# Making twelve features' gate/up weight sums in the mixer, and Strassen down products in the first FFN block

## The chip, the cores and the metric

The kernel runs on one core of one Trainium2 chip. The metric is the device time of one launch in microseconds (us); smaller is better. A time shown for a kernel is the median of several runs.

## The reference, cut to what matters

```python
def hybrid_layer(x, ...):
    h = rmsnorm(x, norm1_w)
    proj = h @ w_in                      # q/k/v, z, a, b, pooling input
    ...                                  # gated delta rule (4 heads) and causal mean pooling (4 groups)
    x = x + concat([o_delta, o_pool]) @ w_out
    h = rmsnorm(x, norm2_w)
    x = x + (silu(h @ w_gate) * (h @ w_up)) @ w_down
    return x, ...
```

There is one layer, 2048 new tokens of a prompt and 64 tokens of a running stream (2112 in all), model width 1024 and FFN width 2816, all in float32. The kernel cuts the FFN width into 22 "features" of 128 columns.

## The kernel before, in words

**Precision.** Every large product is made of three TensorE products: an operand is split into a high part (a copy rounded to float32r, on ScalarE) and a low part (operand less high part, on VectorE); high times high, high times low and low times high are summed in PSUM. "Splitting" a tile is this pair of instructions, one on each engine.

**The mixer** is the first part of the program. It takes the tokens in four blocks of 512 (the first also holds the 64 stream tokens). The loop at lines 1375 to 1436 makes a block's projections head by head, runs the delta-rule chains of the heads beside them, and a block's output projection (`out_proj`, line 1291) is made during the next block. The weights of the projections are split once, kept in DRAM (`wnd`, `wod`) and loaded as 512 KB tiles `wsp` afterwards.

**The FFN** takes the tokens in three blocks of 704, numbered 0, 1 and 2. For each feature `gate_up` (line 1514) computes gate and up with a 2x2 Strassen scheme of seven products. It needs seven weight tiles: three are blocks of the weights as they are (`11`, `12`, `22`), four are sums (`S1` to `S4`). `prep_strassen` (line 582) makes them. In block 0 it loads four raw quarters of 256 KB (`wr`, `wrS`), makes the four sums on GpSimd, splits all seven tiles and stores the four split sums to DRAM (`gsd`, 512 KB each, "gS" in the trace). In blocks 1 and 2 the key is in `stored`, so it loads the four split sums (`wsS<-gS`), and only three raw quarters are loaded and split.

**Down.** The features form six groups of 4, 4, 4, 4, 2 and 4 (`FGROUPS`). A group's down product is made soon after its last gate/up. It has two forms, chosen by `plain` (line 504):

- the plain form (`down`, line 1561): eight weight tiles of 256 KB are loaded and split; each output tile takes, for each half of the tokens, three products per feature, so a group of four takes 8 x 2 x 4 x 3 = 192 matmuls, and VectorE adds 16 results to `y`. `gate_up` splits each feature's result itself.
- the Strassen form (`down_strassen`, line 1595, with `prep_down`, line 616, and `factors`, line 1572): pairs of features are combined, GpSimd makes four sums for a pair of features and four half-width sums for each of four weight tile pairs, more tiles are split, and a group of four takes 4 x 7 x 2 x 3 = 168 matmuls and 28 adds to `y`.

Before the change `SDOWN = (1, 2)`: block 0 uses the plain form everywhere, blocks 1 and 2 the Strassen form (block 2's last group is plain).

**What sets the order.** Nothing goes to the chip as it is written. `Machine` (line 59) records every instruction with the tiles that it reads and writes, and `issue` (line 183) makes one list schedule of the whole program: for each engine it picks, at each planned time, the ready instruction of lowest rank. Rank is the place in the program less `machine.boost`. Planned durations are in `cost` (line 140); a transfer counts as ready for its user 3 us after its planned landing (`MARGIN`); SyncE's transfers whose rank is far ahead of the front are held back until the planned wire is idle (`BACKLOG, IDLE, AHEAD_OPS`). A `Chain` (line 379) is a generator stepped by a rough TensorE clock, which sets where in the program its instructions stand. All transfers are issued by SyncE, in one order; each engine then runs its list in order.

Tiles come from pools with a fixed number of buffers per tag: `wraw` (four raw weight tiles), `wsp` (four split tiles, for projections and FFN alike), `op` (two, large), and the FFN's own pool `f2`, which opens when the mixer's pools `cp1` and `gp` are done.

Of the kernel before, what the change touches and what calls it, by code (L numbers as in the profile page):

```python
# [11 lines left out]
F32 = mybir.dt.float32  # L12
F32R = mybir.dt.float32r
AF = mybir.ActivationFunctionType
ALU = mybir.AluOpType
# [3 lines left out]
P = 128  # L19
# [21 lines left out]
TB2 = NTOK // NB2  # L41
# [3 lines left out]
SUBS2 = ((0, N2), (N2, N2))  # L45
FGROUPS = (4, 4, 4, 4, 2, 4)

SDOWN = (1, 2)

FW = ("11", "S1", "S2", "12", "S3", "S4", "22")  # L50
FH = ("11", "T1", "T2", "21", "T3", "22", "T4")
# [304 lines left out]
def hybrid_kernel(ctx, tc, a, o):  # L356
    nc = machine = Machine(tc.nc)
    act = nc.scalar.activation
    tt = nc.vector.tensor_tensor
# [72 lines left out]
    cpool, wpool, opool = pool("cpool"), pool("wpool"), pool("opool")  # L432
# [5 lines left out]
    cp1, gp = pool("cp1", p1, True), pool("gp", p1, True)  # L438
# [6 lines left out]
    gsd = {nm: dpool.tile([NF, P, 1024], F32, tag=f"g{nm}", name=f"g{nm}") for nm in KEEP}  # L445
# [49 lines left out]
    groups, f0 = [], 0  # L495
# [4 lines left out]
    def halves(b, gi):  # L500

        return ((0,), (1,)) if (b, gi) == (NB2 - 1, len(groups) - 1) else ((0, 1),)

    def plain(b, gi):
        return b not in SDOWN or len(halves(b, gi)) > 1

    order = []
    for b in range(NB2):
# [9 lines left out]
    ready, due, stored = [], [], set()  # L518
# [217 lines left out]
    def norm_stats(B):  # L736

        if B.j == 1:
            B.r = wpool.tile([P, 512], F32, tag="xc", name="rn1", bufs=XBUFS["xc"])
        else:  # L740
            B.r = cpool.tile([P, TB2], F32, tag="r", name=f"rn{B.j}")
        if B.j == 0:
            for _ in rstd("n1_0", B.r, from_x0, S0, gp, "ext", 4, nc.gpsimd, lambda name: bank(0, name)):
                pass
        else:
            Chain(rstd(f"n1_{B.j}", B.r, stream_x(a["xT"], "xa", B.t0), [(0, B.NB)], gp, "ext", 4, nc.gpsimd))
# [69 lines left out]
    names = {}  # L816
# [474 lines left out]
    def out_proj(B):  # L1291
        acts = [(k, B.o[k]) for k in (4, 5, 6, 7, 0, 1, 2, 3)]

        late = [0] if B.kept else []
        src = stream_x(a["xT"], "xc", B.t0, "xc")
        for ms in ((0, 1), *((m,) for m in range(2, KT))) if B.kept else ((m,) for m in range(KT)):
            ws = [weights("wout", m, *late) for m in ms]
            for lo, n in B.subs:
                xs = [src(m, lo, n) for m in ms]
                pss = [psmm(f"pz{B.j}_{m}_{lo}") for m in ms]  # L1300
                for part in (acts[:4], acts[4:]) if len(ms) > 1 else (acts,):
                    for w, ps in zip(ws, pss):
# [23 lines left out]
    def stats2(b, pool, tag, tbufs):  # L1326
# [18 lines left out]
        for k in range(4):  # L1345
# [20 lines left out]
            put("T4", k, t4)  # L1366
            yield LAT_APPLY

    heads = []
    blocks = []  # L1370
    prev = None
    for j in range(NBLK):
        first = None
        if j:
            pab, first = project(B, 0, 1)
        else:
            pab = project(B, 0)
        machine.boost = HOT_ROWS
        rows(B, pab)
        machine.boost = 0  # L1380
        blocks.append(B)
        nxt = Block(j + 1) if j + 1 < NBLK else None
        B.heads, B.pools = [], []
        if prev is None or nxt is None:
            new_o(B)
        for h in range(NH):
            B.heads += head_project(B, h, first if h == 0 else None)
            heads.append(B.heads[h])
            if h == 1 and nxt is None:
                pools(B)  # L1390
            if h == OUT_AFTER and prev is not None and nxt is not None:
                drain(lambda: all(g.done for g in prev.heads) and all(c.done for c in prev.pools))
                out_proj(prev)
                if not B.kept:
                    new_o(B)
            if h == 1 and j == 0:
                fold = Chain(fold_pool())
            if h == 1 and nxt is not None:
                norm_stats(nxt)
            if h == STATS0 and nxt is None:  # L1400
                stats0 = Chain(stats2(0, gp, "ext", 4))
        if j == 0:
            fold.wait()
        if nxt is not None:
            pools(B)
            norm_apply(nxt)
        prev, B = B, (nxt if nxt is not None else B)
# [23 lines left out]
    for k in (4, 5, 6, 7, 0, 1, 2, 3):  # L1431
        t = wpool.tile([P, 512], F32, tag="xc", name=f"od{k}", bufs=XBUFS["xc"])
        nc.sync.dma_start(out=t, in_=od[k])
        split(last_prev.o[k], slice(0, last_prev.NB), t)
    machine.boost = 0
    out_proj(last_prev)
    stats0.wait()
    hA = [bp.tile([P, 6, 2, N2], F32R, tag=f"h{i}", name=f"hA{i}") for i in range(2)]
# [75 lines left out]
    def gate_up(b, f):  # L1514
        w = weights("gu", f)
        tag = f"{b}_{f}"
        raw = f2.tile([P, 2, N2], F32, tag="hr", name=f"hr{tag}", bufs=3)

        def add(ps, nw, nh, first=False):

            for i, t in enumerate(hq[nh]):
                ks = slice(i * P, (i + 1) * P)
                for q, (wi, ai) in enumerate(((0, 0), (0, 1), (1, 0))):
                    mm(ps, w[nw][:, wi, ks], t[:, ai, :], start=first and i == q == 0, stop=i == 3 and q == 2,
                       skip_group_check=not first)
                pump()

        def sigmoid(e, x):
            act(e, x, AF.Exp, scale=-1.0)
            act(e, e, AF.Ln, bias=onec)  # L1530
            act(e, e, AF.Exp, scale=-1.0)

        def finish(i, g, u):
            e = raw[:, i]
            tt(e, e, g, ALU.mult)
            tt(e, e, u, ALU.mult)
            if b not in SDOWN:
                split(h3t[f % 6], slice(i * N2, (i + 1) * N2), e)


        x, y, z = (psg(f"p{i}_{tag}")[:, :N2] for i in "xyz")
        add(x, "11", "11", True)
        hurry(nc.scalar.copy, g1 := tmp(f"g1_{tag}"), x)
        add(y, "S1", "T1", True)
        hurry(nc.scalar.copy, u2 := tmp(f"u2_{tag}"), y)
        add(x, "S2", "T2")
        hurry(nc.scalar.copy, g2 := tmp(f"g2_{tag}"), x)
        add(z, "12", "21", True)
        hurry(tt, g1, z, g1, ALU.add)
        sigmoid(raw[:, 0], g1)  # L1550
        add(x, "S3", "T3")
        hurry(tt, u2, x, u2, ALU.add)
        add(y, "S4", "22")
        hurry(tt, g2, y, g2, ALU.add)
        sigmoid(raw[:, 1], g2)
        finish(1, g2, u2)
        add(x, "22", "T4")
        finish(0, g1, x)
        return raw if b in SDOWN else h3t[f % 6]

    def down(b, gi, h3, ys, which, done):
        f0, G = groups[gi]
# [48 lines left out]


    fpos = {2: (0, 1), 4: (0, 2, 1, 3)}
    six = [opool.tile([P, 3, 2, TB2], F32R, tag="op", name=f"h3_{i}", bufs=2) for i in range(2)]
    h3t = [six[i // 3][:, i % 3] for i in range(6)]
    h3, ys = {}, {}

    def between(b):
# [7 lines left out]
    for op in order:  # L1626
        b = op[1]
        if op[0] == "gu":
            f = op[2]
            if f == 0:  # L1630
                fill.finish()
            if op == ("gu", 0, 2):
                nxt = Chain(between(-1))
            h3[f] = gate_up(b, f)
            if b in SDOWN:
                gi = max(g for g, (f0, G) in enumerate(groups) if f0 <= f)
                if plain(b, gi):
                    if f == groups[gi][0] or f == groups[gi][0] + 2:
                        two = opool.tile([P, 2, 2, TB2], F32R, tag="op", name=f"h3l{f}", bufs=2)
                    for i in range(2):  # L1640
                        split(two[:, f % 2], slice(i * N2, (i + 1) * N2), h3[f][:, i])
                    h3[f] = two[:, f % 2]
                elif f % 2:
                    h3[f] = factors(b, f, h3.pop(f - 1), h3[f])
            if f == NF - 1 and b + 1 < NB2:
                nxt.finish()
                fill = Chain(load_h(b + 1, FH))
        else:
            f0, G = groups[op[2]]
            while b not in ys:  # L1650
                nxt.step()
            hs = [h3.pop(f0 + i) for i in range(G) if f0 + i in h3]
            if not plain(b, op[2]):
                down_strassen(b, op[2], hs, ys[b])
            for which in halves(b, op[2]) if plain(b, op[2]) else ():
                done = []
                if which != (0, 1):
                    Chain(last_norm(b, ys[b], *which, done))
                down(b, op[2], hs, ys[b], which, done)
            if op[2] == len(groups) - 1 and b + 1 < NB2:  # L1660
                nxt = Chain(between(b))
# [33 lines left out]
KEEP = ("S1", "S2", "S3", "S4")  # L1695
HOT_ROWS = BOOST
HPOOL = (0, 1, 2, 3)
LAT_LOAD = 0.6
WAIT_STAT = 8.46

# [111 lines left out]
```

## Time and profile before

| | |
|---|---|
| median of 3 runs | 2340.63 us (2338.54 to 2341.11) |
| the profiled execution's own time | 2338.61 us |
| its span in the trace | 2336.8 us |
| TensorE busy | 2301.8 us, 99% of the span |
| VectorE, ScalarE, GpSimd busy | 72%, 58%, 36% |
| moved by DMA | 471.36 MB, 202 GB/s over the span |

PE stands for TensorE's matmuls and PEld for its weight loads, DVE for VectorE, ACT for ScalarE, POOL for GpSimd, SP or SPq for SyncE's queue. Rows of a group of instructions read: line, engine, operation, output tile <- input tiles, shapes, count | busy us, mean ns of one | idle time of the engine before them and what ended it. Nearly all instructions have line 278, where the scheduler issues them, so one goes by tile names. Rows of a stretch of time read: its limits, its length, then for each engine the busy us with the number of instructions, the granted TensorE clock, the DMA engines' busy share and GB/s.

### The profile page before, as it was taken

To read this page: it belongs to the slowest core of one execution; us is meant where nothing else is said; L and a number is where in the kernel's file an instruction comes from. 1 tells how busy PE (TensorE), PEld (TensorE's weight loads), DVE (VectorE), ACT (ScalarE), POOL (GpSimd) and SP (SyncE) were. 2 spreads that over 40 slices of the span, in tenths; PEclk is the share of its full clock that TensorE was granted. 3 is DMA by queue.
4 is the path that set the end of the run, shared out by engine and by line. 5 is a ranking of instruction groups with operands and counts; after the bars stand their busy time and mean duration, and the time that the engine had idled before them with its cause. 6 is when DMAs were issued, how large, how long until landed. Compare 5 with 4: busy or idle time off the path is not lost.

```text
span 2336.8 us, 41455 instructions
## 1 busy us (share of the span) xinstructions
PE 2301.8 (99%) x14614; PEld 2138.4 (92%) x14614; DVE 1689.0 (72%) x3097; ACT 1356.4 (58%) x3020; POOL 843.6 (36%) x963
## 2 busy tenths in 40 slices
PE   8999999999999999999999999999999999999998
PEld 7898898778777878999999999999999999999998
DVE  8998755664676786788667665877877868766776
ACT  6987856683767675655445465554444664454444
POOL 3434222430234530554322244643432653331312
PEclk9999999999999999999999999999999999999999
DMA  8755566545464577877545377768545586455453
GB/s 293 250 160 181 169 229 209 182 156 192 165 212 159 185 206 239 294 274 252 205 169 187 139 247 231 240 205 285 181 142 183 175 289 220 146 182 189 145 193 105
DMA packets 218881, 471.36 MB, mean 202 GB/s; under 512 B 27184, under 2 KB 85552, under 8 KB 218672
## 3 DMA queue, kind: packets, MB, share of 16 engines
q1 hardware_dynamic: 218672, 468.71, 60.9%
q8 instruction: 115, 1.88, 0.3%
q14 instruction: 94, 0.77, 0.1%
HBM read 354.81 MB, written 113.80 MB: 201 GB/s over the span
## 4 chain that ended last, share of the span: by engine, by line
PE 82%; DVE 9%; ACT 4%; DMA 3%; issue 2%; POOL 0%; SPq 0%; POOLq 0%; DVEq 0%; ACTq 0%
PE px L278 19%; PE pp L278 16%; PE pz L278 12%; PE py L278 8%; PE d L278 8%; PE dx L278 6%; PE dy L278 3%; PE pk_p L278 2%; PE pt_p L278 2%; DVE hq L278 2%; PE dz L278 1%; DVE y L278 1%; PE gr_p L278 1%; PE py_p L278 1%; ACT hr L278 1%
## 5 line engine op out<-in xcount | busy, mean ns | idle before, releaser
L278 PE MATMUL pp<-h,wsp 128*128 128x512 f32 (+1 forms) x2480 | 561.0, 366 | 11.6 <-DVE wsp L278 10.3
L278 PEld LDWEIGHTS pp<-h,wsp 128*128 128x128 f32 x2480 | 400.5, 189 | 59.1 <-ACT wsp L278 8.9
L278 ACT CAST ws<-wr 128x512 fp32r<-128x512 f32 x198 | 122.0, 618 | 172.9 <-PE dx L278 49.6
L278 DVE TENSOR_TENSOR ws<-wr,ws 128x512 fp32r<-128x512 f32 x198 | 164.2, 831 | 57.3 <-ACT ws L278 51.8
L278 PE MATMUL d<-h,wsd 128*128 128x352 f32 x1056 | 170.5, 322 | 0.0
L278 PE MATMUL pz<-op,wsp 128*128 128x288 f32 (+1 forms) x768 | 169.9, 357 | 0.3 <-DVE op L278 0.2
L278 PEld LDWEIGHTS d<-h,wsd 128*128 128x128 f32 x1056 | 168.7, 188 | 0.4 <-DVE h L278 0.4
L278 ACT ACTIVATE hr<-g 128x352 f32<-128x352 f32 x132 | 65.7, 497 | 163.8 <-DVE g L278 163.5
L278 ACT CAST TV_p<-pt_p 128x512 f16<-128x512 f32 x192 | 111.1, 589 | 62.2 <-PE pt_p L278 61.7
L278 PE MATMUL px<-hA,ws 128*128 128x352 f32 x792 | 144.7, 322 | 0.7 <-DVE ws L278 0.7
L278 PE MATMUL py<-hB,wsS 128*128 128x352 f32 x792 | 143.8, 322 | 0.0
L278 PE MATMUL px<-hBT,wsS 128*128 128x352 f32 x792 | 139.6, 324 | 3.0 <-ACT g L278 2.6
L278 PE MATMUL pz<-hB,ws 128*128 128x352 f32 x792 | 142.5, 322 | 0.0
L278 PE MATMUL py<-hA,wsS 128*128 128x352 f32 x792 | 139.8, 322 | 0.0
L278 PE MATMUL px<-hBT,ws 128*128 128x352 f32 x792 | 138.1, 322 | 1.3 <-DVE u L278 1.3
L278 POOL TENSOR_TENSOR wrS<-wr,wrS 128x512 f32<-128x512 f32 x44 | 63.0, 1431 | 207.7 <-DMA wr<-in_wg_dram 64.2
L278 PE MATMUL px<-hA,wsS 128*128 128x352 f32 x792 | 137.8, 322 | 0.0
L278 PEld LDWEIGHTS px<-hBT,wsS 128*128 128x128 f32 x792 | 128.2, 188 | 7.4 <-ACT g L278 7.3
L278 PEld LDWEIGHTS px<-hA,ws 128*128 128x128 f32 x792 | 129.8, 188 | 1.2 <-DVE ws L278 1.0
L278 PEld LDWEIGHTS px<-hBT,ws 128*128 128x128 f32 x792 | 128.6, 188 | 2.3 <-DVE u L278 2.2
L278 PEld LDWEIGHTS py<-hB,wsS 128*128 128x128 f32 x792 | 129.8, 188 | 0.0
L278 PEld LDWEIGHTS pz<-hB,ws 128*128 128x128 f32 x792 | 129.6, 188 | 0.0
(686 smaller groups left out, 5606.3 us busy)
## 6 DMA issues: line engine op xcount, KB each, us to landing
wsS<-gS SPq DMA_DIRECT2D x176, 512.0 KB, 4.6
wsp<-wnd SPq DMA_DIRECT2D x126, 512.0 KB, 3.4
gS<-wsS SPq DMA_DIRECT2D x88, 512.0 KB, 4.4
wr<-in_wg_dram SPq DMA_DIRECT2D x132, 256.0 KB, 3.1
wnd<-wsp SPq DMA_DIRECT2D x42, 512.0 KB, 5.0
xd<-x2d SPq DMA_DIRECT2D x96, 176.0 KB, 3.8
wr<-in_wu_dram SPq DMA_DIRECT2D x66, 256.0 KB, 3.6
wrd<-in_wd_dram SPq DMA_DIRECT2D x56, 256.0 KB, 3.6
```

The costliest lines, as they stand in the source:

```text
L278: getattr(getattr(self.nc, op.eng), name)(*args, **kw)
```

## The change

A new generator `sums_ahead` makes and splits, for features 0 to 11 (`NPRE = 12`), the four sums during the mixer and stores them in `gsd`. It starts in the second token block, after the third head's projections were recorded, and is finished before the last `out_proj`. All its engine instructions and stores have `boost = -1500` (a later rank); each of its steps waits 4 us of the rough clock. It uses the four `wraw` buffers, a new single buffer `sa`, and the space of the constant `poolw`.

For these features block 0 then finds the key in `stored` and loads the split sums, as blocks 1 and 2 do. In block 0 the first three groups (features 0 to 11) use the Strassen down form; the last three stay plain. The tiles `h3t` of the plain form are allocated when first needed (feature 12) rather than ahead of the FFN.

```diff
-SDOWN = (1, 2)
+SPLIT0 = 3
...
     def plain(b, gi):
-        return b not in SDOWN or len(halves(b, gi)) > 1
+        return (b == 0 and gi >= SPLIT0) or len(halves(b, gi)) > 1
...
+    def sums_ahead():
+        gt = nc.gpsimd.tensor_tensor
+        for f in range(NPRE):
+            raw = {}
+            for src, nm, i in (("11", "wg", 0), ("21", "wu", 0), ("22", "wu", 1), ("12", "wg", 1)):
+                raw[src] = wpool.tile([P, 512], F32, tag="wraw", name=f"sa{src}_{f}", bufs=4)
+                nc.sync.dma_start(out=raw[src], in_=a[nm][f][:, i * 512 : i * 512 + 512])
+            yield LAT_SUMS
+            s1, s2, s3, s4 = raw["22"], raw["11"], raw["21"], raw["12"]
+            for i, (nm, out, x, y, op) in enumerate((
+                    ("S1", s1, raw["21"], raw["22"], ALU.add), ("S3", s3, raw["11"], raw["21"], ALU.subtract),
+                    ("S2", s2, s1, raw["11"], ALU.subtract), ("S4", s4, raw["12"], s2, ALU.subtract))):
+                machine.boost = -IDLE_RANK
+                gt(out=out, in0=x, in1=y, op=op)
+                machine.boost = 0
+                if nm != "S1":
+                    yield LAT_SUMS
+            for i, (nm, t) in enumerate((("S1", s1), ("S3", s3), ("S2", s2), ("S4", s4))):
+                machine.boost = -IDLE_RANK
+                if i % 2:
+                    hi = names["poolw"].bitcast(F32R)
+                else:
+                    hi = gp.tile([P, 512], F32R, tag="sa", name=f"sa{nm}_{f}", bufs=1)
+                nc.scalar.copy(hi, t)
+                tt(t.bitcast(F32R), t, hi.bitcast(F32), ALU.subtract)
+                for q, x in enumerate((hi.bitcast(F32), t)):
+                    nc.sync.dma_start(out=gsd[nm][f][:, 512 * q : 512 * q + 512], in_=x)
+                machine.boost = 0
+                yield LAT_SUMS
+            stored.add(("gu", f))
...
+            if (j, h) == (1, 2):
+                ahead = Chain(sums_ahead())
...
     machine.boost = 0
+    ahead.finish()
     out_proj(last_prev)
...
     def gate_up(b, f):
...
+        six = b == 0 and f >= groups[SPLIT0][0]
+        if six and not h3t:
+            h3t.extend(t[:, i] for t in (opool.tile([P, 3, 2, TB2], F32R, tag="op", name=f"h3_{i}", bufs=2) for i in range(2)) for i in range(3))
...
-            if b not in SDOWN:
+            if six:
                 split(h3t[f % 6], slice(i * N2, (i + 1) * N2), e)
...
-            if b in SDOWN:
-                gi = max(g for g, (f0, G) in enumerate(groups) if f0 <= f)
+            gi = max(g for g, (f0, G) in enumerate(groups) if f0 <= f)
+            if b or gi < SPLIT0:
                 if plain(b, gi):
...
+NPRE, IDLE_RANK, LAT_SUMS = 12, 1500, 4.0
```

More of the change, by code (lines that the diff above doesn't have):

```diff
@@ L1558, in gate_up @@
         finish(0, g1, x)
-        return raw if b in SDOWN else h3t[f % 6]
+        return h3t[f % 6] if six else raw
     def down(b, gi, h3, ys, which, done):
@@ L1613, in hybrid_kernel @@
     fpos = {2: (0, 1), 4: (0, 2, 1, 3)}
-    six = [opool.tile([P, 3, 2, TB2], F32R, tag="op", name=f"h3_{i}", bufs=2) for i in range(2)]
-    h3t = [six[i // 3][:, i % 3] for i in range(6)]
+    h3t = []
     h3, ys = {}, {}
```

## The prediction

> **What bounds the kernel now.** I read the page's head first, then busy time by stage, then the rate of TensorE's matmuls in each FFN block, then the waits.
>
> ```profile
> span 2336.8 us, 41455 instructions
> PE 2301.8 (99%) x14614; PEld 2138.4 (92%) x14614; DVE 1689.0 (72%) x3097; ACT 1356.4 (58%) x3020; POOL 843.6 (36%) x963
> ...
> PE 82%; DVE 9%; ACT 4%; DMA 3%; issue 2%; POOL 0%; SPq 0%; POOLq 0%; DVEq 0%; ACTq 0%
> ```
>
> TensorE is busy for 99% of the span and makes up 82% of the chain that ended last. The timeline of PE gives the borders of the FFN blocks: the first `px` matmul of blocks 0, 1 and 2.
>
> ```profile
> 946.10 2.08 PE L278 MATMUL px<-hA,ws 128*128 128x352 f32 x12
> ...
> 1414.34 2.08 PE L278 MATMUL px<-hA,ws 128*128 128x352 f32 x12
> ...
> 1867.83 1.61 PE L278 MATMUL px<-hA,ws 128*128 128x352 f32 x9
> ```
>
> The table by stretches then has the mixer's middle and the blocks 0 and 1:
>
> ```profile
> 330.00:820.00 490.00, 488.52 (x2977) 391.79 (x2975) 300.47 (x607) 312.03 (x749) 165.06 (x238) 1.00 0.57 186
> 946.10:1414.30 468.20, 466.95 (x2909) 465.28 (x2908) 332.87 (x511) 242.77 (x490) 182.52 (x142) 1.00 0.64 222
> 1414.30:1867.80 453.50, 448.57 (x2770) 443.03 (x2769) 348.91 (x595) 236.73 (x497) 193.89 (x199) 1.00 0.63 203
> ```
>
> In block 0 PE idles 1.25 of 468.2 us, and a matmul takes 468.2 / 2909 = 0.1610 us from start to start. In block 1, which already has what the change brings to block 0 (stored sums, Strassen down), it is 453.5 / 2770 = 0.1637 us. So time in the FFN is the number of matmuls, plus a little waiting that the Strassen form brings. In the mixer's middle PE idles 1.5 of 490 us. The clock is 1.00 in all three, so no term comes from it.
>
> **Part 1: fewer matmuls in block 0.** A group of four takes 168 instead of 192 matmuls; three groups remove 72. These are the ones removed:
>
> ```profile
> L278 PE MATMUL d<-h,wsd 128*128 128x352 f32 x1056 | 170.5, 322 | 0.0
> ```
>
> 170.5 / 1056 is 0.1615 us each, in agreement with block 0's rate, and no idle time stands before them. 72 x 0.1610 = **-11.6 us**. PE is the path here, so all of it counts.
>
> **Part 2: what the Strassen form gives back.** The three groups bring pair sums and weight sums on POOL, more splits on ACT and DVE, and 36 more adds to `y` on DVE, while 48 sums and their splits leave block 0. I need not add these up, since block 1 shows the finished mixture: DVE 348.9, ACT 236.7 and POOL 193.9 us of 453.5, no engine over 77%. What counts is the waiting that it causes. At block 1's rate the remaining 2909 - 72 = 2837 matmuls would take 2837 x 0.1637 = 464.5 us, and the gain would be only 3.7; at block 0's rate 11.6. These are the two ends. Block 1's surplus is 2770 x 0.0027 = 7.6 us. The waits of PE in 1414 to 1868 say where it is from, as far as they are named, and the timeline where two of them stand:
>
> ```profile
> PE px L278 <- ACT g L278: 1.8, 6, 0.5
> PE dz L278 <- DVE hq L278: 1.1, 1, 1.1
> PE dz L278 <- DVE y L278: 1.1, 2, 0.5
> PE dy L278 <- DVE y L278: 0.7, 1, 0.7
> ```
>
> ```profile
> 1845.98 0.43 PE L278 MATMUL dz<-hq,wsd 128*128 128x352 f32 x1 [1.07 <-DVE hq L278]
> ...
> 1860.35 1.23 PE L278 MATMUL dz<-hq,wsd 128*128 128x352 f32 x6 [0.54 <-DVE y L278]
> ```
>
> The waits of `dz` and `dy`, 2.9 us together, belong by these rows to the end of the block, where features run out and down products stand back to back; block 0's end stays plain. What is left, 4.7 us, I share by features: 12 of 22 is 2.6, and I take **+2.5 us** (ends 0 and 7.9). It is ScalarE's copy of `px` (`g`) coming late behind the splits of the pair tiles.
>
> **Part 3: what the mixer pays.** `sums_ahead` adds 48 sums on POOL, 48 copies on ACT, 48 subtractions on DVE, 48 loads and 96 stores of 256 KB. The same work in block 0 has these rows; the transfers are compared with loads of the same size:
>
> ```profile
> L278 POOL TENSOR_TENSOR wrS<-wrS,wr 128x512 f32<-128x512 f32 x44 | 63.8, 1451 | 29.6 <-DMA wr<-in_wu_dram 12.7 <-DVE hr L278 6.8 <-DVE wsS L278 5.8
> L278 POOL TENSOR_TENSOR wrS<-wr,wrS 128x512 f32<-128x512 f32 x44 | 63.0, 1431 | 207.7 <-DMA wr<-in_wg_dram 64.2 <-DMA wrS<-in_wu_dram 58.9 <-DMA xc<-in_xT_dram 29.2
> L278 ACT CAST wsS<-wrS 128x512 fp32r<-128x512 f32 x88 | 53.3, 618 | 82.8 <-PE d L278 55.5 <-POOL wrS L278 10.9 <-PE px L278 5.7
> L278 DVE TENSOR_TENSOR wsS<-wrS,wsS 128x512 fp32r<-128x512 f32 x88 | 78.7, 902 | 21.6 <-ACT wsS L278 20.9
> ```
>
> ```profile
> wr<-in_wg_dram SPq DMA_DIRECT2D x132, 256.0 KB, 3.1
> ```
>
> POOL 48 x 1.44 = 69 us, ACT 48 x 0.618 = 30, DVE 48 x 0.902 = 43. In the order of the changed kernel these stand beside instructions that began between about 324 and 818 us before, so I lay them on the 490 us of the mixer's middle: DVE 300.5 + 43 = 344 (70%), ACT 312 + 30 = 342 (70%), POOL 165 + 69 = 234 (48%). The transfers are 144 x 0.262 = 37.7 MB, 77 GB/s over 490 us, so 186 becomes 263 GB/s. Are such loads bearable? The trace has stretches of the mixer as full or fuller:
>
> ```profile
> 100.00:200.00 100.00, 99.75 (x858) 92.73 (x857) 91.99 (x220) 85.90 (x223) 43.31 (x71) 1.00 0.58 183
> 450.00:500.00 50.00, 50.00 (x315) 40.64 (x314) 37.71 (x82) 39.26 (x94) 18.26 (x26) 1.00 0.48 160
> 650.00:700.00 50.00, 48.97 (x300) 39.67 (x299) 38.08 (x71) 31.74 (x69) 20.46 (x29) 1.00 0.68 221
> 800.00:850.00 50.00, 48.60 (x296) 35.93 (x295) 42.66 (x87) 42.43 (x111) 24.03 (x27) 1.00 0.70 199
> 900.00:950.00 50.00, 50.00 (x229) 42.01 (x228) 38.17 (x62) 27.21 (x56) 8.31 (x6) 1.00 0.86 277
> ```
>
> With DVE at 92% and ACT at 86% (100 to 200) PE idles 0.25 us in 100; with 277 GB/s (900 to 950) not at all. But 650 to 700 and 800 to 850 lose 2.1% and 2.8% at DVE 76% and 85%. Ends: below, the 1.5 us of idle time that PE has there could vanish, -1.5; above, all 490 us at the loss of 800 to 850, 13.7 - 1.5 = +12.2. The nearest row by load is 450 to 500 (DVE 75%, ACT 79%, POOL 37%, no loss). I stay near it, but let the idle time grow from 0.3% to 0.8%, since the added instructions also stand in front of others on three in-order engines: **+2.5 us**. What is queued behind them are evictions (`ext`), the delta chains' small steps on DVE and POOL, and on SyncE the loads of `wsp`; dense matmuls of the next block, which need none of the small steps, are what PE does meanwhile.
>
> SyncE issues 144 transfers more in the mixer and 12 fewer in block 0. Its queue has the time; the rows are its longest wait in 330 to 820, and two groups of transfers:
>
> ```profile
> SPq L278 <- PE pp L278: 240.3, 82, 6.0
> ```
>
> ```profile
> gS<-wsS SPq DMA_DIRECT2D x88, 512.0 KB, 4.4
> wsS<-gS SPq DMA_DIRECT2D x176, 512.0 KB, 4.6
> ```
>
> 240 us of the mixer's middle it waits for a free `wsp` buffer. In block 0, 48 loads of split sums replace 48 stores of the same size, and 12 raw loads go; block 1 lives with the loads. At the FFN's start the first sums are no longer made from raw quarters but loaded, 4.6 us, when a `wsp` buffer comes free; I put this at nothing, covered by the twelve matmuls of `px` from `hA`; uncovered it costs one landing, some 2 us, inside part 2's ends.
>
> **The skill's rule on the port.** One row shows what moving GpSimd's sums may do to VectorE; the columns are ns, minimum, median and maximum:
>
> ```profile
> L278 DVE TENSOR_TENSOR wsS<-wrS,wsS x88: 674/693/1840, 940.5 to 1369.2; 128x512 fp32r<-128x512 f32 x88
> ```
>
> A subtraction that mostly takes 0.69 us sometimes takes 1.84: longer by about one GpSimd sum. The Trainium skill, "SBUF — State Buffer", section "SBUF: two separate sides", says that a VectorE instruction with two SBUF inputs and a GpSimd instruction hold the same port pair by an exclusive lock for the whole instruction; the row agrees. By that rule the change takes 69 us of locked port out of an FFN block with slack and puts it into the mixer, among the delta chains' small steps.
>
> **Sum.** -11.6 + 2.5 + 2.5 = -6.6 us. Against the profiled execution's own 2338.61 (the span of 2336.8 and 1.8 around it) this is 2332.0. That execution is 2.0 below the median of the runs, 2340.63, to which I apply the sum: **2334.0 us**, 0.28% faster. About 0.2%, 4.7 us, is what a measurement of this kernel can tell from no change.
>
> **Rivals.**
>
> *Full gain:* the mixer hides all, and block 0 keeps its rate: -11.6, 2329.0. For it: 100 to 200 and 450 to 500. Against it: part 2's waits. 0.08.
>
> *Strassen waits eat it:* block 0 takes on all of block 1's rate: -3.7 + 2.5 = -1.2, 2339.4, no change. For it: identical code. Against it: block 1's waits at its end, which block 0 does not get. 0.12.
>
> *The port:* the sums hold VectorE up in the mixer. Up to 69 us more on DVE would make 413 of 490, 84%, as in 800 to 850; then the mixer loses at the share of 650 to 700 (+8.5) or 800 to 850 (+12.2): -9.1 + 8.5 to 12.2 is -0.6 to +3.1, so 2340.0 to 2343.7, no change. Against it: 100 to 200. 0.14.
>
> *Weights late behind the stores, slower than before:* 144 transfers of 0.262 MB, 0.95 us of wire each at 277 GB/s, now share the queue with the mixer's loads of weights:
>
> ```profile
> wsp<-wnd SPq DMA_DIRECT2D x126, 512.0 KB, 3.4
> ```
>
> As SPq waits for PE to free a buffer, these are issued at the last moment, and a store ahead of one delays it. If PE must wait the 0.95 us for about 15 of them, part 3 reaches 13.8 and the kernel is slower by 0.2%; for 25 it is 23.8 - 9.1 = +14.7, 2355.3. Against it: 900 to 950, and the planner's place for the stores, when the wire is idle. 0.10.
>
> That the change does not do what it says I exclude: the order of the changed kernel has 72 matmuls fewer on PE.
>
> **How the numbers follow.** Forecast 0.56 (2331 to 2337), the rivals 0.08, 0.12, 0.14 and 0.10. Faster takes the forecast's main part and the full gain, 0.62; the forecast's upper edge is within 0.2% (over 2335.9), with the second and third rival 0.28; slower 0.10. The range, 2328.5 to 2342, takes in the full gain, the forecast, the second rival and the lower half of the third.
>
> **What would show it.** In the trace after, the first `px` of block 1 less that of block 0 should be about 459 us (468.2 - 9.1), with some 2837 matmuls; near 456.6 is the full gain, near 464.5 the second rival. The first `px` of block 0 should stand at about 948.5 instead of 946.1; at 955 or more with long DVE instructions the port is right, with PE waiting for `wsp` loads the last rival. Blocks 1 and 2 should keep their 453.5 and 469 us within 1; a change there would be a mistake of this text.

## The result and the profile after

| | before | after |
|---|---|---|
| median | 2340.66 us (10 runs, 2338.54 to 2342.22) | 2346.49 us (10 runs, 2344.86 to 2347.89) |
| ratio to before | 1 | 1.0025, 95% interval 1.0017 to 1.0034 |
| the profiled execution's own time | 2338.61 | 2345.28 |

The change makes the kernel 5.8 us slower, 0.25%. The forecast was 6.6 us faster.

The head of the page of the kernel after, in the order in which that of before was read:

```profile
span 2343.5 us, 41836 instructions
PE 2299.4 (98%) x14542; PEld 2129.7 (91%) x14542; DVE 1756.4 (75%) x3175; ACT 1375.1 (59%) x3062; POOL 923.1 (39%) x1035
...
PE 75%; DVE 12%; ACT 5%; DMA 4%; issue 3%; POOL 1%; SPq 0%; DVEq 0%; POOLq 0%; ACTq 0%
```

The 72 matmuls are gone (14614 to 14542), yet PE's busy time fell by only 2.4 us, and on the chain that ended last 7% moved away from PE: 3 to DVE and 1 each to ACT, DMA, POOL and issue. The timeline of PE gives the borders, the first `px` of the three blocks:

```profile
958.58 1.60 PE L278 MATMUL px<-hA,ws 128*128 128x352 f32 x9
...
1420.29 2.08 PE L278 MATMUL px<-hA,ws 128*128 128x352 f32 x12
...
1870.64 0.32 PE L278 MATMUL px<-hA,ws 128*128 128x352 f32 x1
```

So the FFN starts 12.5 us late; block 0 is 461.7 us long (before 468.2, 6.5 less); blocks 1 and 2 together have 923.2 (before 922.5). 12.5 - 6.5 + 0.7 = 6.7, which is 2345.28 - 2338.61. **The change saves in block 0 and pays twice that in the mixer.** The mixer from 330 us to the first FFN matmul, of before:

```profile
330.00:946.10 616.10, 613.22 (x3685) 492.13 (x3684) 395.92 (x786) 389.75 (x922) 192.05 (x265) 1.00 0.60 194
```

and of after, with its stretches and the two blocks:

```profile
330.00:958.60 628.60, 619.62 (x3689) 494.86 (x3688) 454.88 (x830) 413.43 (x966) 269.86 (x309) 0.99 0.79 252
...
450.00:500.00 50.00, 49.23 (x289) 38.10 (x288) 44.02 (x84) 39.17 (x92) 25.57 (x30) 1.00 0.77 244
...
800.00:850.00 50.00, 46.03 (x251) 35.22 (x250) 46.40 (x74) 36.36 (x85) 31.36 (x33) 0.96 0.76 222
...
958.60:1420.30 461.70, 457.49 (x2838) 453.92 (x2837) 338.14 (x545) 238.18 (x488) 185.75 (x170) 1.00 0.64 216
1420.30:1870.60 450.30, 445.79 (x2753) 440.59 (x2753) 346.73 (x588) 235.44 (x494) 189.30 (x196) 1.00 0.63 202
```

VectorE has 59 us more, of which its 48 subtractions are 42; the rest is older instructions that take longer. 450 to 500, my nearest row, now runs 289 matmuls instead of 315. PE idles 9.0 of 628.6 us instead of 2.9; its longest waits are, by name, for the engines that work for the chains and for `od`, none for `wsp` (the list of PE's waits of over 0.1 us in this stretch has no load):

```profile
PE pz L278 <- ACT op L278: 1.8, 1, 1.8
PE py_p L278 <- ACT TV_p L278: 1.8, 3, 1.1
PE po_p__2203 L278 <- DVE osq_p__2195 L278: 1.2, 1, 1.2
PE pt_p L278 <- DVE Yt_p L278: 1.0, 2, 0.8
```

That VectorE is held up beside a sum is seen in the timeline: two sums on GpSimd, and three instructions of VectorE that take 1.33 us each, where the mean before was 0.77.

```profile
474.69 3.47 POOL L278 TENSOR_TENSOR sa<-sa,sa 128x512 f32<-128x512 f32 x2
475.51 3.99 DVE L278 SCALAR_TENSOR_TENSOR Yvz<-ext,consts,Yvz 128x512 f32<-128x512 f32 x3
```

Over the whole stretch from 330 us to the FFN two such groups of VectorE's instructions take 947 and 1055 ns on the mean, before 847 and 773 (rows of before stand in the fourth group):

```profile
L278 DVE SCALAR_TENSOR_TENSOR Yqk<-ext,consts,Yqk 128x512 f32<-128x512 f32 x60 | 56.8, 947 | 5.1 <-ACT Yqk L278 4.4
...
L278 DVE SCALAR_TENSOR_TENSOR Yvz<-ext,consts,Yvz 128x512 f32<-128x512 f32 x30 | 31.7, 1055 | 3.9 <-ACT Yvz L278 3.4
```

**Where the mixer pays.** A delta chain's small steps and the dense matmuls share PE. As long as projections (`pp`) are left, PE has something to do when a chain step is late. The timeline of PE in the kernel before, where the projections end:

```profile
830.74 1.40 PE L278 MATMUL pp<-h,wsp 128*128 128x512 f32 x5
...
832.33 0.44 PE L278 MATMUL ptk_p<-consts,Yqk 128*128 128x128 f32 x2
832.86 1.13 PE L278 MATMUL gr_p<-Yqk 128*128 128x256 f32 x4
```

and in the kernel after (in brackets how long PE was idle before, and for what):

```profile
834.66 1.64 PE L278 MATMUL pp<-h,wsp 128*128 128x512 f32 x6
...
837.76 0.27 PE L278 MATMUL py_p<-TV_p,Wh_p 128*128 128x128 f16 x2 [1.12 <-ACT TV_p L278]
...
848.41 0.73 PE L278 MATMUL pz<-op,wsp 128*128 128x512 f32 x2 [1.81 <-ACT op L278]
...
853.80 0.60 PE L278 MATMUL ptk_p<-consts,Yqk 128*128 128x128 f32 x4
...
859.29 0.59 PE L278 MATMUL gr_p<-Yqk 128*128 128x256 f32 x2
```

The last `pp` comes 4 us later, but the chain's next `ptk_p` and `gr_p`, which before stood right behind it, 21 and 26 us later: the chains are late, and that shows only when the projections have run out. From the start of the last `pp` matmul to the first FFN matmul it is 114.3 us before (831.8 to 946.1) and 122.7 after (835.9 to 958.6). So 8.4 of the 12.5 us are lost in this **tail**, and 4.1 ahead of it. Behind the last `pp` stand 244 matmuls of the chains before and 272 after (counted in the traces, all ahead of the FFN that are neither `pp` nor `pz`). Of the 8.4 us PE's idle time in the tail is 3.0 (1.4 before, 4.4 after), two stretches at half the granted clock, shown in the last section, are 3.4, and the 28 matmuls more are, by an estimate from their rate before, 1.8.

### The profile page after: what moved, and what is told of

Read it like the earlier page. It is cut to its first block, busy times and chain, and to the rows that moved or that the text cites. A ratio compares the mean times of both kernels' runs of the same rounds, so it can differ in the third digit from the quotient of the medians.

```text
span 2343.5 us, 41836 instructions
## 1 busy us (share of the span) xinstructions
PE 2299.4 (98%) x14542; PEld 2129.7 (91%) x14542; DVE 1756.4 (75%) x3175; ACT 1375.1 (59%) x3062; POOL 923.1 (39%) x1035
## 4 chain that ended last, share of the span: by engine, by line
PE 75%; DVE 12%; ACT 5%; DMA 4%; issue 3%; POOL 1%; SPq 0%; DVEq 0%; POOLq 0%; ACTq 0%
PE px L278 17%; PE pp L278 14%; PE pz L278 11%; PE py L278 7%; PE dx L278 7%; PE d L278 4%; PE dy L278 4%; DVE hq L278 2%; PE dz L278 2%; DVE y L278 2%; PE pk_p L278 2%; PE pt_p L278 1%; PE gr_p L278 1%; DVE Yqk L278 1%; PE py_p L278 1%
## 5 line engine op out<-in xcount | busy, mean ns | idle before, releaser
L278 POOL TENSOR_TENSOR q<-hr,hr 128x352 f32<-128x352 f32 x52 | 58.2, 1120 | 293.1 <-DVE hr L278 223.9
L278 DVE TENSOR_TENSOR y<-y,dx 128x352 f32<-128x352 f32 x224 | 113.1, 513 | 31.2 <-PE dx L278 29.9
L278 PEld LDWEIGHTS pz<-op,wsp 128*128 128x128 f32 x768 | 121.0, 192 | 13.1 <-ACT op L278 2.2
```

Source lines behind the costliest of these rows:

```text
L278: getattr(getattr(self.nc, op.eng), name)(*args, **kw)
```

## Experiments

Theories: **lock**: GpSimd's sums hold up VectorE, which makes the chains late; **load**: any work on VectorE does; **transfers**: the 144 DMAs do; and, for where it is paid, **debt**: the tail grows with the chain matmuls left in it; against **place**: any changed order loses there. Times are medians; each group has its own runs of the kernel before (2340.62, 2341.27, 2340.29, 2339.93 and 2339.85 us). "FFN starts" is the first FFN matmul, 946.1 us before. Starts, stretches and tails are from the one traced execution of each kernel, and its own time can lie up to 5 us from the median (e18 5.0 above, e6, e8 and e12 3 above, e17 2.9 below).

### First group: which part

e1, the Strassen form without the sums ahead:

```diff
-NPRE, IDLE_RANK, LAT_SUMS = 12, 1500, 4.0
+NPRE, IDLE_RANK, LAT_SUMS = 0, 1500, 4.0
```

> The Strassen down products of three groups in block 0, with no sums made in the mixer (their sums are made in block 0 as before the change). If the mixer's added work alone costs the 12.5 us by which block 0 starts later (946.1 before, 958.6 after), block 0 starts at 946 to 947 here. For block 0 itself: theory 1, that 72 fewer matmuls are worth about what the changed kernel shows (468.2 to 461.7 us), gives block 0 some 461 us and a total of 2334 us, faster than before by 0.28%. Rival: with the sums still in block 0, GpSimd (182 + 72 us) and VectorE (333 + 50 us of some 457) are too full, block 0 takes 468 us or more, and the total is 2341 or more.

e2, the sums ahead without the Strassen form:

```diff
-SPLIT0 = 3
+SPLIT0 = 0
```

> The sums in the mixer, stored and loaded by block 0, but plain down products in all of block 0. Theory 1 (the mixer pays for the sums whatever block 0 does with them): block 0 starts at 958 to 959, and takes 466 to 468 us, total 2351 to 2353. Rival: the list schedule of the whole program differs, and the later start is a chance of that one order: block 0 starts anywhere from 947 to 955.

e3 has the transfers alone; SPLIT0 = 0, nothing is entered in `stored`, and the raw quarters are stored (block 0 then makes its sums as before and overwrites them, in e4 to e6 too):

```diff
-                gt(out=out, in0=x, in1=y, op=op)
-                nc.scalar.copy(hi, t)
-                tt(t.bitcast(F32R), t, hi.bitcast(F32), ALU.subtract)
-                for q, x in enumerate((hi.bitcast(F32), t)):
+                for q, x in enumerate((t, t)):
-            stored.add(("gu", f))
```

> Plain down products, the sums made in block 0 as before, and in the mixer only the 48 loads and 96 stores of sums_ahead, without its sums, copies and subtractions (what it stores is raw quarters, overwritten in block 0). Theory A (the port and the added engine work hold the delta chains up): block 0 starts at 946 to 949, total 2341 to 2344. Theory B (the transfers make other transfers late, the od loads above all): block 0 starts at 953 to 958, total 2348 to 2353.

e4 leaves out the stores alone, FFN as before:

```diff
-                for q, x in enumerate((hi.bitcast(F32), t)):
-                    nc.sync.dma_start(out=gsd[nm][f][:, 512 * q : 512 * q + 512], in_=x)
-            stored.add(("gu", f))
```

> As e3, but the mixer has the 48 loads with all sums, copies and subtractions, and none of the 96 stores (the results are dropped). Theory A (port and engine work): block 0 starts at 953 to 958, total 2348 to 2353. Theory B (transfers): block 0 starts at 946 to 949, total 2341 to 2344. If both have a share, e3 and e4 each start block 0 in between, at 949 to 953.

Measured: e1 2358.04 us (1.0071, 1.0056 to 1.0087), e2 2350.52 (1.0041, 1.0026 to 1.0056), e3 2345.57 (1.0021, 1.0012 to 1.0030), e4 2359.61 (1.0078, 1.0061 to 1.0095). The FFN starts at 947.0 in e1 and at 959.7 in e2: what the mixer pays comes with the sums ahead, whatever form block 0 has. Block 0 in e1 and e2, by stretches:

```profile
947.00:1433.10 486.10, 467.38 (x2837) 457.03 (x2837) 403.20 (x589) 259.10 (x532) 261.00 (x214) 0.99 0.63 214
```

```profile
959.70:1425.70 466.00, 466.00 (x2909) 465.56 (x2908) 273.13 (x467) 220.11 (x446) 114.76 (x98) 1.00 0.65 213
```

With the sums gone from it, block 0 in e2 has no idle time at all and gains 2.2 us (468.2 to 466.0); the Strassen form then takes it to 461.7, 4.3 less, where 72 matmuls of 0.160 us are 11.5. So the Strassen form gives back 7.2 us. In e1, without the sums ahead, it makes block 0 18 us longer (POOL 261 us, DVE 403): it needs them. The mixer in e3, and in e4:

```profile
330.00:950.10 620.10, 615.08 (x3688) 491.86 (x3687) 401.03 (x787) 389.27 (x922) 193.91 (x265) 1.00 0.80 253
```

```profile
330.00:964.50 634.50, 619.96 (x3685) 494.95 (x3685) 453.22 (x834) 410.94 (x970) 267.09 (x313) 0.99 0.65 208
```

At 253 GB/s, the rate of the changed kernel, the transfers alone start the FFN 4.0 us late, between the two forecasts; the engine work with the loads but without the stores 18.4, above both. The transfers are the smaller part, and the parts do not add up.

### Second group: whose work

e5 leaves out the sums on GpSimd, e6 the copies and subtractions; otherwise as e3 (plain form, raw quarters split and stored; sums stored unsplit):

```diff
-                gt(out=out, in0=x, in1=y, op=op)
+                pass
```

> As e3 (plain down, sums made in block 0), but the mixer's generator has its 48 loads, 48 copies on ScalarE, 48 subtractions on VectorE and 96 stores, without the 48 GpSimd sums (raw quarters are split and stored, overwritten in block 0). Theory A1 (the lock of the port by the GpSimd sums is what counts): block 0 starts at 950 to 953, near e3's 950.1. Theory A2 (the load on the in-order ScalarE and VectorE counts): block 0 starts at 955 to 959, near e2's 959.7.

```diff
-                nc.scalar.copy(hi, t)
-                tt(t.bitcast(F32R), t, hi.bitcast(F32), ALU.subtract)
```

> The counterpart of e5: loads, the 48 GpSimd sums and 96 stores, without copies and subtractions (unsplit sums are stored, overwritten in block 0). Theory A1 (port): block 0 starts at 955 to 959. Theory A2 (load on ScalarE and VectorE): block 0 starts at 950 to 953.

e7 is the changed kernel with the mixer's sums on VectorE:

```diff
-        gt = nc.gpsimd.tensor_tensor
+        gt = nc.vector.tensor_tensor
```

> The changed kernel with the 48 sums in the mixer made by VectorE, so that GpSimd no longer holds the port for them (GpSimd 69 us less, VectorE some 33 us more). Theory A1 (port): block 0 starts at 951 to 955, total 2339 to 2343. Theory A2 (load): block 0 starts at 959 to 963, total 2347 to 2351. The length of block 0 stays at 462 us in both.

e8 is the changed kernel with the store of `out_cprompt` (12-byte pieces, ahead of the reads of `od` in SyncE's order) made to wait for a late tile:

```diff
+    late = cp1.tile([P, 12, 3], F32, tag="late", name="late")
+    stt(late, Sp[:, 0, :36].rearrange("p (m t) -> p m t", t=3), 0.0, chist, ALU.mult, ALU.add)
-    for nm, t in (("cprompt", chist), ("pprompt", phist), ("csamp", shist), ("psamp", sphst)):
+    for nm, t in (("cprompt", late), ("pprompt", phist), ("csamp", shist), ("psamp", sphst)):
```

> The changed kernel with one transfer moved: the store of the convolution state (out_cprompt, 12-byte pieces), which in the changed kernel is issued at 838.2, 1.3 us ahead of the od loads that the last output projections wait for, takes a copy made late as its source and is issued behind them. If those small pieces are what makes the od loads land after 8 us instead of 4, the loss of 4.1 us between 845 and 871 goes, the clock does not fall at 850, block 0 starts at 954 to 955 and the total is 2342 to 2343. Rival: the od loads are late for another reason (weights and x2d loads in the queue), block 0 starts at 957 to 960 and the total stays at 2345 to 2348.

Measured: e5 2351.67 us (1.0047, 1.0031 to 1.0064), e6 2356.68 (1.0068, 1.0053 to 1.0083), e7 2350.30 (1.0039, 1.0024 to 1.0054), e8 2343.43 (1.0010, 1.0001 to 1.0019). The mixer in e5, e6 and e7:

```profile
330.00:954.60 624.60, 617.36 (x3694) 494.51 (x3694) 433.72 (x836) 414.11 (x971) 200.59 (x265) 1.00 0.80 252
```

```profile
330.00:963.30 633.30, 622.65 (x3692) 495.53 (x3691) 425.98 (x787) 388.55 (x923) 267.75 (x313) 0.99 0.78 248
```

```profile
330.00:965.10 635.10, 621.36 (x3695) 492.05 (x3695) 469.51 (x880) 410.67 (x967) 200.66 (x261) 1.00 0.79 250
```

GpSimd's sums (e6 against e3) cost 13.2 us by the FFN's start, 10.5 by the medians, and VectorE, without an instruction more than in e3 (787 in each), is busy 25 us longer. The splits (e5 against e3) cost 4.5. e5's start lies between its two forecasts, those of e6 and e7 above both of theirs. And e7, without any of these sums on GpSimd, loses 19.0: the lock is not the only way to lose. In e8 the reads of `od` land sooner; the issues of DMAs in after and in e8 (KB, us from issue to landing):

```profile
od<-od SPq DMA_DIRECT2D x8, 256.0 KB, 6.1
```

```profile
od<-od SPq DMA_DIRECT2D x8, 256.0 KB, 4.3
```

Before it was 3.5. e8 is 3 us under after in time, but its traced execution is the slowest of its ten (2346.45) and starts the FFN no earlier (959.0). Where its 3 us come from is not shown.

### Third group: how much work, and sums by themselves

e9, e10 and e11 move eight, four and eight features, with as many groups in Strassen form (two, one, two); e11 has e8's edit as well:

```diff
-SPLIT0 = 3
+SPLIT0 = 2
-NPRE, IDLE_RANK, LAT_SUMS = 12, 1500, 4.0
+NPRE, IDLE_RANK, LAT_SUMS = 8, 1500, 4.0
```

> Sums of eight features in the mixer, two groups with Strassen down in block 0; everything is still computed. The sums then end near 650 us, well before the stretch of 790 to 871 us where the changed kernel lost 7 of its 12.5 us. Theory A (the added work itself, where it stands beside the delta chains, makes the waits): the mixer loses what the changed kernel had lost by about 650 us, 4 to 6, so block 0 starts at 950 to 952; block 0 gains two thirds of 6.5, so is 464 long; 2340.7 + 5 - 4.3 + 0.5 = about 2342. Theory B (the losses stand at the mixer's end in any changed plan): block 0 starts at 955 or later, with waits of PE and a half clock between 835 and 860 as before; about 2346.

> Sums of four features, one group with Strassen down in block 0; everything is still computed. The sums end near 480 us, ahead of every loss that the changed kernel showed. Theory A: the mixer loses 0 to 2, block 0 starts at 946 to 948 and is 466 long; 2340.7 + 1 - 2.2 = about 2339.5, no change. Theory B: the mixer loses 4 or more, at its end, block 0 starts at 950 or later; 2343 or more.

> The run with eight features, with the store of the convolution's prompt state issued behind the reads of od. If that store slows the reads of od whatever stands before it, this run is 1 to 3 us under the run with eight features, without a half clock at 840 to 860: about 2340. If the store only mattered in the changed kernel's plan, the two are equal within 1.

e12 replaces the body of `sums_ahead` (plain form in block 0):

```diff
+        pw = names["poolw"]
+        for f in range(4 * NPRE):
+            machine.boost = -IDLE_RANK
+            s = gp.tile([P, 512], F32, tag="sa", name=f"sa{f}", bufs=1)
+            gt(out=s, in0=pw, in1=pw, op=ALU.add)
+            machine.boost = 0
+            yield 2 * LAT_SUMS
```

> Plain down in block 0 and no sums stored, so the FFN is that of before; the mixer has only 48 additions on GpSimd of a constant with itself, into one private tile that nobody reads: no loads, no stores, no splits (the output is whole). If GpSimd's sums alone hold VectorE up, VectorE's other instructions in 330 to the start of block 0 take some 20 us longer (396 becomes 410 to 420), and the mixer loses 5 or more: 2346 or more. If the loss needs the transfers or the splits beside the sums, the mixer loses less than 3: about 2342.

Measured: e9 2349.71 us (1.0041, 1.0029 to 1.0054), e10 2346.45 (1.0033, 1.0021 to 1.0046), e11 2350.74 (1.0042, 1.0028 to 1.0056), e12 2367.55 (1.0119, 1.0106 to 1.0133). In e9 the FFN starts at 956.3, 10.2 late: 3.7 ahead of the last `pp`, about as theory A had it, and 6.5 behind it, as B had it, though the sums were long over. Block 0 gains nothing (468.4 us, with 6.8 us at half the granted clock). In e10 it starts only 3.4 late, but block 0 is 473.9 us long, 5.7 longer than before, with 6.8 us at half the clock (3.4 us of work) in an execution 2.7 above the median: with the sums of the other 18 features still in it, one Strassen group saved nothing. e11 equals e9 within 1.1, so e8's edit is of no use in that order.

e12 did not test what it should: its sums need nothing, so the order put them at the start of the program, at 25 to 147 us. What they cost there is plain, though. 25 to 150 us in before, and in e12:

```profile
25.00:150.00 125.00, 123.01 (x981) 114.00 (x980) 114.70 (x260) 100.62 (x256) 54.44 (x94) 1.00 0.68 234
```

```profile
25.00:150.00 125.00, 109.45 (x758) 99.16 (x757) 109.44 (x193) 77.33 (x187) 103.75 (x119) 0.93 0.60 207
```

58 us of sums (GpSimd's busy time on `sa`) beside a VectorE that was at 92% before leave 223 matmuls undone, some of them by a clock of 0.93: the FFN starts 31.7 us late.

### Fourth group: lock or load, debt or place

e13 is e12 with sums that wait for a load, so that they stand in the mixer's middle; e14 the same on VectorE:

```diff
+        for f in range(NPRE):
+            raw = wpool.tile([P, 512], F32, tag="wraw", name=f"sa11_{f}", bufs=4)
+            nc.sync.dma_start(out=raw, in_=a["wg"][f][:, :512])
+            for k in range(4):
+                yield 2 * LAT_SUMS
+                machine.boost = -IDLE_RANK
+                s = gp.tile([P, 512], F32, tag="sa", name=f"sa{k}_{f}", bufs=1)
+                nc.gpsimd.tensor_tensor(out=s, in0=raw, in1=raw, op=ALU.add)
+                machine.boost = 0
```

> FFN as before. The mixer has only 48 additions on GpSimd, paced as the sums of the changed kernel, of a loaded quarter with itself into a tile that nobody reads, and 12 loads of 256 KB; no splits, no stores (the output is whole). Theory lock (GpSimd's sums hold VectorE up and with it the delta chains): VectorE's busy time from 330 us to the first FFN matmul is 405 to 420 instead of 396 without an instruction more, and the FFN starts 5 to 13 us late; 2346 to 2354. Theory transfers (the sums hurt only beside 144 transfers): the FFN starts at most 3 late; under 2344.

> The same, with the 48 additions on VectorE: some 33 us of work more on VectorE, nothing on GpSimd (the output is whole). Theory lock: VectorE has room (396 of 616 us), the FFN starts at most 3 us late; under 2344. Theory load (what counts is VectorE's time, whoever takes it): 33 us on VectorE cost as much as the lengthening by GpSimd's sums, the FFN starts 4 to 10 late; 2345 to 2351.

e15 begins the changed kernel's sums in the first token block, e16 too, with other constants:

```diff
-            if (j, h) == (1, 2):
-                ahead = Chain(sums_ahead())
...
             fold.wait()
+            ahead = Chain(sums_ahead())
```

```diff
-NPRE, IDLE_RANK, LAT_SUMS = 12, 1500, 4.0
+NPRE, IDLE_RANK, LAT_SUMS = 12, 3000, 4.5
```

> The changed kernel whole, with its sums begun at the end of the first token block instead of in the second. In the order of its instructions 244 of the delta chains' matmuls stand behind the last projection matmul, as in the kernel before; in the changed kernel it is 272. Theory debt (added work delays the chains; the projections' matmuls hide this until they run out near 836 us, and then what the chains are late is paid): between the last projection and 871 us it loses at most 1.5 instead of 4 to 6, the FFN starts at 951 to 955, block 0 is 462 long as in the changed kernel; 2339 to 2343. Theory place (the stretch of 836 to 871 us loses 4 to 6 in any changed order): the FFN starts at 957 or later; 2345 or more.

> The run before this one with the sums at a later rank (3000) and a slower pace (4.5): the same work, begun at the same place, but 264 of the chains' matmuls stand behind the last projection. Theory debt: it loses 3 to 6 us more than the run before this one between the last projection and 871 us. Theory place: both lose the same there, within 1.

Measured: e13 2346.15 us (1.0027, 1.0017 to 1.0037), e14 2340.22 (1.0001, 0.9992 to 1.0010), e15 2371.72 (1.0136, 1.0119 to 1.0153), e16 2378.61 (1.0168, 1.0152 to 1.0183). Two groups of VectorE's own work in the mixer (busy us, mean ns), in before, e13 and e14:

```profile
L278 DVE SCALAR_TENSOR_TENSOR Yqk<-ext,consts,Yqk 128x512 f32<-128x512 f32 x60 | 50.8, 847 | 8.0 <-ACT Yqk L278 7.0
L278 DVE SCALAR_TENSOR_TENSOR Yvz<-ext,consts,Yvz 128x512 f32<-128x512 f32 x30 | 23.2, 773 | 4.2 <-ACT Yvz L278 3.8
```

```profile
L278 DVE SCALAR_TENSOR_TENSOR Yqk<-ext,consts,Yqk 128x512 f32<-128x512 f32 x60 | 55.3, 922 | 10.6 <-ACT Yqk L278 9.6
L278 DVE SCALAR_TENSOR_TENSOR Yvz<-ext,consts,Yvz 128x512 f32<-128x512 f32 x30 | 28.1, 938 | 3.7 <-ACT Yvz L278 3.2
```

```profile
L278 DVE SCALAR_TENSOR_TENSOR Yqk<-ext,consts,Yqk 128x512 f32<-128x512 f32 x60 | 50.1, 836 | 7.2 <-ACT Yqk L278 6.2
...
L278 DVE SCALAR_TENSOR_TENSOR Yvz<-ext,consts,Yvz 128x512 f32<-128x512 f32 x30 | 24.1, 804 | 4.7 <-ACT Yvz L278 4.2
```

55 us of sums on GpSimd alone lengthen VectorE's work (414 us busy from 330 us to the FFN, within lock's forecast), and the kernel takes 6 us more; 35 us of the same additions on VectorE itself cost nothing. For work by itself, lock has the direction right and load falls. But of e13's 6 us only 3.4 are in the FFN's start, between the two forecasts; 3.2 are in block 0, which is 471.4 us long though its work is that of before; why stays open. And e13's sums stand closer together, from 341 to 433 us, than the changed kernel's, 350 to 792.

In e15 the sums begin at 199 us, where VectorE has less room, and the run misses its forecast by 30 us: 150 to 330 us has 1237 matmuls instead of 1360. But the fourth group was made for the tail. All 20 kernels, by the matmuls of the chains behind the last `pp`:

| chain matmuls left | tail in us |
|---|---|
| 244 | before 114.3, e1 115.9, e10 115.4, e12 114.5, e13 114.3, e14 115.4, e15 116.0 |
| 248 | e17 118.1, e18 118.1 |
| 254 | e3 117.7, e7 119.8, e9 120.8, e11 120.3 |
| 260 | e6 120.4 |
| 264 | e4 118.2, e5 120.7, e16 122.2 |
| 272 | after 122.7, e2 123.2, e8 121.9 |

e15 and e16 do the same work; with 20 chain matmuls more in it (1.3 us of PE's time at the rates of before) e16's tail is 6.2 us longer, just above what debt foretold (3 to 6). Place falls: a changed order with 244 left, like e15 or e13, loses at most 1.7, and that is one stretch at half the clock.

Three limits. Less the time lost to the clock, the tails of 244 are 113.7 to 114.5 us and all those of 254 to 272 are 117.7 to 120.7, so among the latter the count orders nothing. The count is fixed by the planner's order ahead of the run: e13, with the 244 of before, has before's tail, though VectorE is busy 18 us longer there. And the tail needs no lock: e5, without a sum on GpSimd, has 6.4 of the 8.4 us, e3, with transfers alone, 3.4.

### Fifth group: other places for the same work

e17 and e18, the changed kernel whole with, first and second:

```diff
-NPRE, IDLE_RANK, LAT_SUMS = 12, 1500, 4.0
+NPRE, IDLE_RANK, LAT_SUMS = 12, 500, 0.5
```

```diff
-            if (j, h) == (1, 2):
+            if (j, h) == (1, 3):
-NPRE, IDLE_RANK, LAT_SUMS = 12, 1500, 4.0
+NPRE, IDLE_RANK, LAT_SUMS = 12, 0, 2.0
```

> The changed kernel whole, with its sums paced at 0.5 instead of 4 and a rank 500 instead of 1500 later: the same work, over earlier. 248 of the chains' matmuls stand behind the last projection (before 244, changed kernel 272). Theory debt: from the last projection on it loses 1 to 2.5 us instead of the changed kernel's 5 to 6; if the rest of the mixer loses its 6 to 7 as there, the FFN starts near 955 and the time is about 2342.5. If work packed more densely costs the chains more directly, as when it began earlier, the FFN starts at 958 or later; 2346 or more.

> The changed kernel whole, with its sums begun one head later, at a pace of 2 and with no later rank: again 248 chain matmuls behind the last projection. Theory debt: 1 to 2.5 us lost from the last projection on. The rest of the mixer is not foretold by it: 5 to 15 us, so 2341 to 2352.

Measured: e17 2354.54 us (1.0065, 1.0052 to 1.0077), e18 2352.40 (1.0051, 1.0038 to 1.0065). The tails lie above those of 244, at the lower end of those of 254, 3.8 over before (I had expected 1 to 2.5). But the last `pp` now comes 15.6 and 20.5 us late, against 4.1 in after: the sums' last start is at 665 and 695 us, against 792, and packed more densely they seem to hurt the chains at once. None of the runs beats the kernel before.

## Why the prediction was wrong

- **Part 1, right.** 72 matmuls of 0.160 us went (2909 to 2838 rows in block 0).
- **Part 2, mis-sized.** The forecast was -11.6 + 2.5 = -9.1; block 0 became 6.5 shorter. Moving the sums out gave 2.2 (e2), which I had not counted, and the Strassen form gave back 7.2, not 2.5. By my second bound, block 1's whole rate, the block would have been 464.5; it was 461.7, about half way from my 459.1 to that bound. I had put part of block 1's waits down to its end.
- **Part 3, the step that failed.** I took +2.5 from the row of 450 to 500 in before, with the reason that dense matmuls of the next block need none of the small steps. It was 12.5, just above my upper end of 12.2. Two things were wrong. The engines' shares in a stretch of before said nothing about what added work does to the instructions beside it, by the lock (e13) or without it (e5, e7). And the dense matmuls do not remove a delay of the chains, they only put it off: 8.4 of the 12.5 us fall due in the tail, after the last sum (its start is at 792 us). A stretch without loss was no evidence that the work there was free.
- **The rivals.** "The port" came nearest: slower than forecast, FFN start over 955 with long VectorE instructions, 8.5 to 12.2 us of mixer loss. I had given it 0.14 and ended it at 2343.7 because I kept part 2's full -9.1. As a mechanism it holds for the sums by themselves (e13, e14, e6), but e7 shows that it is not all. The Trainium skill, "SBUF — State Buffer", section "SBUF: two separate sides", has an exclusive lock between GpSimd and a VectorE instruction with two SBUF inputs; e13 and e14 agree, by the mean of `Yvz` above (773 ns before, 938 with GpSimd's sums, 804 with VectorE's). "Weights late behind the stores" fell: in the mixer of after no wait of PE for a load of `wsp` is among those named, and the transfers alone cost 4.0.
- **Blocks 1 and 2.** I had them at 453.5 and 469 within 1; they are 450.3 and 472.9. Block 1 has 2753 matmul rows instead of 2770 and block 2 has 2838 instead of 2822: some 16 matmuls, 2.6 us, moved behind the border. Their sum moved by 0.7.

Left open: why the parts do not add up, and so how much of the 12.5 us is the lock. Each of e4, e6 and e7 loses more than the changed kernel does with all of the work, with different orders by the planner, and 11 to 15 us of it ahead of the tail. A list schedule that is made anew for each kernel changes more than the part taken out: without the stores the last sum starts at 607 us instead of 792. In e7 it still starts at 793, so closeness is not all.

## What to carry to other kernels

Filler work hides a late chain of small steps only until the filler ends; before moving work "under" it, look at the place where the filler runs out and count what of the chain is left there, in the order of the instructions, ahead of any run. The count is coarse: it told 244 from 254 and more, and nothing finer. A stretch that loses nothing may be running up that debt. And price work moved beside a busy VectorE by what it does to VectorE's own instructions: by itself it lengthened them on GpSimd (e13) and cost nothing on VectorE (e14), but beside splits and transfers the move to VectorE did not help (e7).

## What the hardware showed that I had not expected

Short idling of TensorE was followed by half the granted clock. Stretches of 2 us in the kernel after:

```profile
836.00:838.00 2.00, 0.88 (x13) 0.63 (x12) 1.91 (x5) 1.97 (x5) 0.00 (x0) 1.00 0.36 102
838.00:840.00 2.00, 1.34 (x13) 0.82 (x10) 2.00 (x4) 2.00 (x5) 0.00 (x0) 0.86 0.90 246
840.00:842.00 2.00, 2.00 (x7) 1.61 (x6) 2.00 (x5) 1.56 (x4) 0.00 (x0) 0.50 1.19 184
...
850.00:852.00 2.00, 2.00 (x6) 1.19 (x6) 1.89 (x4) 2.00 (x5) 0.00 (x0) 0.50 0.91 304
```

From 836 to 840 PE idled 1.8 us, the longest gap 1.12 us, and the clock was 0.50 for 3.4 us from 839.4 on, and again from 849.7 after the gap of 1.81; each such stretch costs 1.7 us of work, about as much as the gap itself. Before has none from 330 us to the FFN. The Trainium skill, "TensorE: Matmul & The Clock Gate", section "Part 1: The HAM clock gate (the "warmup" mystery)", counts on an idle window of about 3.4 us before the clock falls; here single gaps were at most 1.12 and 1.81 us, and PE was busy for 59% and 47% of the 3.4 us ahead of each fall. The length of a gap does not decide: in e7 a gap of 1.60 us, up to 853.2, had no fall behind it, and in e14 the clock fell at 837.8 us with no gap over 0.9 us.

All 33 falls between 150 and 2200 us in the 20 traces stand, within their trace, on a grid of 3.413 us. Each of the 21 stretches of that grid in which PE was busy for less than half was followed by a fall. From there to 72% twelve were and some 60 were not, above that none was; what decides there stays open.
